# A recurrent decoder layer on one core: fifteen weight tiles split anew in every block instead of stored as parts, and neighbouring rows of w_in on a partition

## The chip, the core and the metric

The kernel runs on one core of one Trainium2 chip. The metric is the device time of one execution in microseconds (us). Five engines work side by side: PE (TensorE: matmuls, with its weight loads shown as PEld), DVE (VectorE), ACT (ScalarE), POOL (GpSimd) and SP (SyncE, which here only issues transfers); 16 DMA engines move the data. Each engine takes its instructions in the order of its own queue.

## The reference

One layer of a decoder on 2048 prompt tokens and 8 x 8 sample tokens. The input is normalised, one product with `w_in` (1024 x 8208) gives everything else, two branches (an RG-LRU with a causal convolution, and a gated delta rule) run over it, each is projected by its own matrix (`w_br_lru`, `w_br_gdn`), the two are weighed by sigmoid merge gates `m_lru`, `m_gdn` that are themselves 2 x 1024 columns of the input product, and `w_out` ends it.

```python
u = rms_norm(x, norm_pre)
z = jnp.einsum('btd,de->bte', u, w_in)
lru_x, lru_gate, gdn_qkv, gdn_gate, gdn_b, gdn_a, m_lru, m_gdn = jnp.split(z, offsets, axis=-1)
...
lru_out = h.astype(x.dtype) * jax.nn.silu(lru_gate)
...
p_lru = jnp.einsum('bte,ed->btd', lru_out, w_br_lru)
p_gdn = jnp.einsum('bte,ed->btd', gdn_out, w_br_gdn)
merged = jax.nn.sigmoid(m_lru) * p_lru + jax.nn.sigmoid(m_gdn) * p_gdn
y = jnp.einsum('btd,de->bte', merged, w_out)
x_new = x + rms_norm(y, norm_post)
```

All of it is float32. A float32 product is made of three products of a shorter format: each operand is split in a high part and the remainder, `hi` and `lo`, and `hi*hi + hi*lo + lo*hi` is summed (L545, L547, L549 in the kernel).

## The kernel before, in words

The 2048 prompt tokens go in four blocks of 512 (the loop `for blkno`); block 0 also takes the 64 sample tokens, so its moving operand has 576 columns and each weight tile is used in two halves of 256 and 320. In each block the same 88 weight tiles are used in the same order, `worder`. Places 0 to 15 alternate a K tile (one head's keys) and a merge-gate tile; 16 to 30 alternate the eight LRU input tiles and seven more merge-gate tiles; 31 to 34 are LRU gate tiles; 35 to 58 are q, v and gate tiles of the heads; 59 is the sixteenth merge-gate tile, 60 to 63 the other LRU gates, 64 to 79 the tiles of `w_br_gdn` and `w_br_lru`, 80 to 87 those of `w_out`.

A tile in its raw form is 1024 x 128 float32, 512 KB: 128 partitions of 8 rows each. Split, it is 1 MB. The matrices don't fit in the on-chip memory, so they pass through slots: three buffers `whl`, from block 1 on a fourth, `whx`, that takes every fourth tile (`wtile`).

- In block 0 `wload` fetches a raw tile (`raws`, or two neighbouring tiles as one `raw` of 1 MB), `split` (L203) writes `hi` by a Copy on ACT (its line in the profile is the helper's, L143) and `lo` by a subtraction on POOL (L205), and `wstore` (L275) writes the split tile, 1 MB, to a scratch tensor `dW` in DRAM: 88 stores. A tile's store is issued when the next tile is split (`wstore(1)`).
- In blocks 1 to 3 the slots are filled from `dW` (L300): 264 loads of 1 MB.

`proj` is one tile's work on PE: 8 steps of three matmuls. It takes a tile with `nextw`, calls `wfetch` for the tiles ahead, and hands the results to an evacuation on ACT or DVE. In block 0 that call also sets `A.after`: what ACT does next is ordered behind the split of the tile ahead ("weights first"). While the weights pass, PE is filled up with the products of the recurrent parts: `W.pump` doles out tasks by a cost table. What those tasks load and store through DRAM (`dk`, `dM`, `dD`, `dDT`, `er`, `dgc`) goes over SP's queue as well, in the order in which it was written, and so stands between the loads and stores of the weights.

The moving operand is the normalised input, transposed: `u_tile` (L348) turns token rows `ux` into channel rows by PE transposes (L196), eight groups `k` per block, scaled by `npre` as they leave PSUM. Group `k` holds channels `128k` to `128k+127`, as a raw tile holds rows `k*128+p` of `w_in` on partition `p`: the rearrangement in `wload` reads

```python
src[:, c:c + 128].rearrange("(k p) c -> p k c", p=128)
```

and `npre` is made of `norm_pre` by one more transpose at the start (`r0`).

## Time and profile before

| | us |
|---|---|
| three runs | 2682.43, 2687.51 (median), 2694.59 |
| the profiled execution | 2683.57 |
| its span | 2681.9 |
| PE busy (96 % of the span) | 2572.9 |
| DVE busy (56 %) | 1496.9 |
| ACT busy (33 %) | 885.3 |
| POOL busy (21 %) | 566.1 |
| stores `dW<-whl` | 88 of 1024 KB |
| loads `whl<-dW` and `whx<-dW` | 199 and 65 of 1024 KB |

How to read it: busy time is summed per engine, and an engine's idle time costs something only where it is on the path that sets the end. The chain that ended last runs over PE for 67 % of the span. Block 0 ends and block 1 begins at about 880 us; the four blocks are not alike, since only block 0 loads raw weights, splits and stores. The row of the granted TensorE clock over 40 slices reads 9 (90 % or more) nearly everywhere, and 8 in three slices between 134 and 335 us. The DMA row stands at 9 in several slices before 700 us.

### The profile page before, as it was taken

Reading aid. Unit: us, or ns where it says so; the run is one execution under the profiler, and the core shown is the slowest. Engines: PE = TensorE matmul, PEld = TensorE weight load, DVE = VectorE, ACT = ScalarE, POOL = GpSimd, SP = SyncE. Lnnn points to the kernel's source line nnn. Section 1 sums busy time; section 2 is a strip of 40 time slices with the busy share of each in tenths; the row PEclk is TensorE's granted clock in tenths of the full one; section 3 lists DMA queues with packets and bytes.
Section 4 is the critical chain, followed back from the end, with each engine's and each line's share of the span. In section 5 each row is a group of like instructions: output and inputs, shape, how many; then the busy total and the mean of one; then the engine's idle time right before and its main releaser. Section 6 shows DMA issues by size and latency. Waiting matters only on the chain.

```text
span 2681.9 us, 39949 instructions
## 1 busy us (share of the span) xinstructions
PE 2572.9 (96%) x15332; PEld 2238.6 (83%) x15332; DVE 1496.9 (56%) x3441; ACT 885.3 (33%) x1722; POOL 566.1 (21%) x444
## 2 busy tenths in 40 slices
PE   6888799999999999999999999999999999999999
PEld 5887798888999788888889788888889888888888
DVE  4567677787434557566523557566513458566512
ACT  5324543333324225323303235333303235333301
POOL 2443342232540211100110121100210211110200
PEclk9988899999999999999999999999999999999999
DMA  7987988789887887554466796544466886655465
GB/s 191 245 256 196 229 205 186 205 176 178 253 295 262 276 271 232 193 177 158 157 240 253 248 290 220 199 168 158 156 244 258 274 274 217 200 172 167 161 236 200
DMA packets 327897, 581.82 MB, mean 217 GB/s; under 512 B 70849, under 2 KB 236762, under 8 KB 282650
## 3 DMA queue, kind: packets, MB, share of 16 engines
q1 hardware_dynamic: 313882, 553.57, 67.0%
q10 hardware_dynamic: 13824, 25.70, 2.5%
q8 instruction: 121, 1.98, 0.3%
q14 instruction: 70, 0.57, 0.1%
HBM read 421.61 MB, written 157.59 MB: 216 GB/s over the span
## 4 chain that ended last, share of the span: by engine, by line
PE 67%; DMA 3%; issue 2%; DVE 1%; POOL 1%; ACT 1%; SPq 0%; ACTq 0%; POOLq 0%; DVEq 0%
PE mm L549 17%; PE mm L545 16%; PE mm L547 16%; PE g L192 5%; PE c L192 4%; PE mm L1284 2%; PE mm L1286 2%; PE mm L1288 2%; PE g L196 2%; DMA er<-dgc 1%; DMA dE<-er 1%; DMA dgc<-gr 0%; POOL er L746 0%; DVE cvy L576 0%; DMA ux<-in_x_prompt_dram 0%
## 5 line engine op out<-in xcount | busy, mean ns | idle before, releaser
L545 PE MATMUL mm<-a,whl 128*128 128x512 f32 (+2 forms) x2432 | 864.1, 355 | 25.5 <-ACT tmo L143 24.4
L549 PE MATMUL mm<-a,whl 128*128 128x512 f32 (+2 forms) x2432 | 868.7, 357 | 6.1 <-POOL whl L205 6.1
L547 PE MATMUL mm<-a,whl 128*128 128x512 f32 (+2 forms) x2432 | 862.8, 355 | 0.0
L545 PEld LDWEIGHTS mm<-a,whl 128*128 128x128 f32 x2432 | 465.5, 191 | 74.6 <-ACT tmo L143 26.1
L549 PEld LDWEIGHTS mm<-a,whl 128*128 128x128 f32 x2432 | 465.8, 192 | 59.3 <-POOL whl L205 6.7
L547 PEld LDWEIGHTS mm<-a,whl 128*128 128x128 f32 x2432 | 465.3, 191 | 45.8
L576 DVE SCALAR_TENSOR_TENSOR cvy<-cvr,cwg,cvy 128x512 f32<-128x512 f32 x288 | 220.0, 764 | 17.7 <-ACT cvy L143 12.4
L547 PE MATMUL mm<-a,whx 128*128 128x512 f32 x448 | 181.7, 406 | 0.0
L549 PE MATMUL mm<-a,whx 128*128 128x512 f32 x448 | 181.4, 405 | 0.0
L545 PE MATMUL mm<-a,whx 128*128 128x512 f32 x448 | 179.3, 400 | 0.0
L1222 DVE SCALAR_TENSOR_TENSOR pt<-tm,mm 128x512 f32<-128x512 f32 (+1 forms) x80 | 47.4, 592 | 189.6 <-PE mm L549 189.6
L1076 POOL TENSOR_TENSOR st<-st,mhalf 128x4 f32<-128x4 f32 x32 | 32.3, 1009 | 507.8 <-DVE st L1074 496.0
L143 ACT ACTIVATE cvr<-mm 128x512 f32<-128x512 f32 (+1 forms) x160 | 81.6, 510 | 172.3 <-PE mm L549 163.8
L205 POOL TENSOR_TENSOR whl<-raw,whl 128x1024 fp32r<-128x1024 f32 x44 | 108.5, 2467 | 121.4 <-ACT whl L143 107.0
L205 POOL TENSOR_TENSOR whl<-raws,whl 128x1024 fp32r<-128x1024 f32 x36 | 90.1, 2503 | 188.9 <-ACT whl L143 170.9
L1286 PE MATMUL mm<-whl,bt 128*128 128x256 f32 x448 | 126.4, 282 | 0.8 <-DVE whl L205 0.8
L1288 PE MATMUL mm<-whl,bt 128*128 128x256 f32 x448 | 126.3, 282 | 0.6 <-DVE yss L1262 0.6
L1284 PE MATMUL mm<-whl,bt 128*128 128x256 f32 x448 | 126.2, 282 | 0.0
L143 ACT ACTIVATE th<-cvy 128x512 f32<-128x512 f32 (+1 forms) x96 | 61.8, 644 | 188.3 <-DVE cvy L576 128.4
L143 ACT ACTIVATE yv<-c 128x128 f32<-128x128 f32 x128 | 35.5, 278 | 243.0 <-PE c L192 242.5
L549 PE MATMUL mm<-gp,whl 128*128 128x512 f32 (+2 forms) x296 | 104.2, 352 | 0.0
L545 PE MATMUL mm<-gp,whl 128*128 128x512 f32 (+2 forms) x296 | 104.1, 352 | 0.0
(331 smaller groups left out, 4645.9 us busy)
## 6 DMA issues: line engine op xcount, KB each, us to landing
whl<-dW SPq DMA_DIRECT2D x199, 1024.0 KB
dW<-whl SPq DMA_DIRECT2D x88, 1024.0 KB
whx<-dW SPq DMA_DIRECT2D x65, 1024.0 KB
raws<-in_w_in_dram SPq DMA_DIRECT2D x33, 512.0 KB
raw<-in_w_in_dram SPq DMA_DIRECT2D x15, 1024.0 KB
dtm<-tmo ACTq DMA_DIRECT2D x48, 256.0 KB
tm<-dtm SPq DMA_DIRECT2D x48, 256.0 KB
ux<-in_x_prompt_dram SPq DMA_DIRECT2D x16, 512.0 KB
```

The source lines that it names most:

```text
L143: r = f(*args, **kw)
L192: T.matmul(out, a, b, start=start, stop=stop)
L196: T.transpose(out, in_, idn)
L205: (eng or G).tensor_tensor(out=lo, in0=src, in1=hi.bitcast(F32), op=OP.subtract)
L545: T.matmul(ps[:, :n], wh, mh[:, c0:c0 + n], start=k == 0, stop=False)
L547: T.matmul(ps[:, :n], wh, ml[:, c0:c0 + n], start=False, stop=False)
L549: T.matmul(ps[:, :n], lo[:, k, :], mh[:, c0:c0 + n], start=False, stop=k == 7)
L576: V.scalar_tensor_tensor(out=y[:, :TB], in0=raw[:, i:i + TB], scalar=cw[:, i, ti:ti + 1], in1=y[:, :TB], op0=OP.mult, op1=OP.add)
L1222: proj(mov, lambda ps, c0, n: V.scalar_tensor_tensor(out=t_[:, c0:c0 + n], in0=x[:, c0:c0 + n], scalar=1.0, in1=ps[:, :n], op0=OP.add, op1 ...
L1284: T.matmul(ps[:, :256], mh[:, cs], wh[:, k % 4], start=k == 0, stop=False)
L1286: T.matmul(ps[:, :256], mh[:, cs], wl[:, k % 4], start=False, stop=False)
L1288: T.matmul(ps[:, :256], ml[:, cs], wh[:, k % 4], start=False, stop=k == 7)
```

## The change

Fifteen of the sixteen merge-gate tiles (`whole`: `mcol[:15]`, all but the one at place 59) are not stored in block 0. In blocks 1 to 3 they are loaded from `w_in` in raw form, two neighbouring tiles per transfer of 1 MB (the last alone, 512 KB: eight transfers per block), into the buffer `whx`, now called `wraw` there, and split into a `whl` slot again: an ACT Copy and a POOL subtraction per tile, 45 of each in all. `whx` serves no other tile at places up to 35 (`NP1`), and every fourth one behind; the split tiles at places up to 35 have the three `whl` buffers, and `proj` there asks for two tiles ahead and not three. The raw transfer of the next pair is issued by `wfetch` up to three tiles ahead.

Besides, rows of `w_in` are laid out the other way round (`krows`): partition `p` takes the eight neighbouring rows `8p` to `8p+7`, which in DRAM lie 32,832 bytes apart, where before it took rows `p`, `128+p`, and so on, 4,202,496 bytes apart. Each row piece is as long as before (512 bytes for a tile, 1 KB for a pair). So that the products stay the same, `u_tile` transposes every eighth channel of `ux` (a stride of 8 float32 along the row) and not 128 neighbouring ones, and `npre` is loaded directly in that layout; `r0`, its transpose and copy are gone. `w_br` and `w_out` tiles are laid out as before.

```diff
@@ -238,15 +238,20 @@
         wplace.setdefault(key(e), len(wplace))
     dW = [dram.tile([128, 2, 1024], F32, name=f"dW{i}") for i in range(len(wplace))]
     wstores, wraws = [], {}
+    NW, NP1 = len(wplace), paired[1]
+    whole = {key(e) for e in mcol[:8 + LM]}
+
+    def krows(a, by8):
+
+        return a.rearrange("(p k) c -> p k c", k=8) if by8 else a.rearrange("(k p) c -> p k c", p=128)
 
     wready = []
     wlast = [None]
     wnext, lnext = [0], [0]
-    ring, wx = [0], []
-
-    def wtile():
-        ring[0] += 1
-        if wx and ring[0] % 4 == 0:
+    wx = []
+
+    def wtile(n):
+        if wx and n % NW > NP1 and (n % NW - NP1) % 4 == 1:
             return wx[0].tile([128, 2, 1024], F32R, name="whx", tag="whx")
         return wp.tile([128, 2, 1024], F32R, name="whl", tag="whl", bufs=3)
 
@@ -260,15 +265,16 @@
             SP.dma_start(raw, src[c[1] * 512:(c[1] + 1) * 512, c[0] * 256:(c[0] + 1) * 256]
                          .rearrange("(k p) c -> p k c", p=128))
             wraws[key(e)] = raw
-        elif not (paired[0] <= n < paired[1] or paired[2] <= n < paired[3]):
+        elif not wx and not (paired[0] <= n < paired[1] or paired[2] <= n < paired[3]):
             raw = rw.tile([128, 8, 128], F32, name="raws", tag="raws")
-            SP.dma_start(raw, src[:, c:c + 128].rearrange("(k p) c -> p k c", p=128))
+            SP.dma_start(raw, krows(src[:, c:c + 128], src is win))
             wraws[key(e)] = raw
         else:
             two = [key(x) for x in worder[n:n + 7]].count((src.tensor.name, c + 128))
             w = 128 + 128 * two
-            raw = rp[0].tile([128, 8, w], F32, name="raw", tag="raw")
-            SP.dma_start(raw, src[:, c:c + w].rearrange("(k p) c -> p k c", p=128))
+            raw = (wx[0].tile([128, 8, w], F32, name="wraw", tag="whx") if wx else
+                   rp[0].tile([128, 8, w], F32, name="raw", tag="raw"))
+            SP.dma_start(raw, krows(src[:, c:c + w], src is win))
             for j in range(1 + two):
                 wraws[src.tensor.name, c + 128 * j] = raw[:, :, 128 * j:128 * j + 128]
 
@@ -279,13 +285,14 @@
             SP.dma_start(dW[i], hl.bitcast(F32))
 
     def wfetch(ahead):
+
 
         while wnext[0] < len(worder) and len(wready) < ahead:
             n = wnext[0]
             e = worder[n]
             place = wplace[key(e)]
             out = isinstance(e[1], tuple)
-            hl = wtile()
+            hl = wtile(n)
             hi, lo = (hl[:, j].rearrange("p (k c) -> p k c", c=256 if out else 128) for j in range(2))
             if n < len(wplace):
                 while lnext[0] < len(wplace) and lnext[0] <= n + (
@@ -294,10 +301,21 @@
                     lnext[0] += 1
                 wstore(1)
                 wlast[0] = split(hi, lo, wraws[key(e)], V if out else None)
-                wstores.append((place, hl))
+                if key(e) not in whole:
+                    wstores.append((place, hl))
+            elif key(e) in whole:
+                wstore()
+                wload(n)
+                split(hi, lo, wraws.pop(key(e)))
             else:
                 wstore()
                 SP.dma_start(hl.bitcast(F32), dW[place])
+            if wx:
+                for j in range(n + 1, min(n + 4, len(worder))):
+                    if key(worder[j]) in whole:
+                        if not any(x in wraws for x in whole):
+                            wload(j)
+                        break
             wready.append((hi, lo))
             wnext[0] += 1
 
@@ -351,7 +369,7 @@
             t = gtile()
             n = 0
             for xt, m in grp:
-                tr(t[:, n:n + m], xt[:m, k * 128:(k + 1) * 128], ident[:m, :m])
+                tr(t[:, n:n + m], xt[:m].rearrange("t (p k) -> t k p", k=8)[:, k], ident[:m, :m])
                 n += m
             cs = slice(gi * 512, gi * 512 + n)
             act(hi[:, cs], t[:, :n], AF.Copy, scale=npre[:, k:k + 1])
@@ -411,14 +429,10 @@
     with tc.tile_pool(name="init", bufs=2, side="right") as ip:
         rows = lambda a: a.rearrange("o (g p) -> (o g) p", p=128)
         with tc.tile_pool(name="u0", bufs=1) as up:
-            r0 = ip.tile([8, 128], F32, name="r0")
-            SP.dma_start(r0, rows(norm_pre))
+            SP.dma_start(npre, norm_pre.rearrange("o (p k) -> (o p) k", k=8))
             xh = u_load(0, up)
-            t = gtile()
-            tr(t[:, :8], r0, ident[:8, :8])
-            V.tensor_copy(npre, t[:, :8])
             wraw = ip.tile([128, 8, 16], F32, name="wraw", bufs=1)
-            SP.dma_start(wraw, win[:, C_B:C_B + 16].rearrange("(k p) c -> p k c", p=128))
+            SP.dma_start(wraw, krows(win[:, C_B:C_B + 16], True))
             u_norm(xh, up)
             zz = ip.tile([128, 96], F32, name="zz", bufs=1)
             V.memset(zz, 0.0)
@@ -526,7 +540,7 @@
         if blkno == 1:
             rw_cm.__exit__(None, None, None)
             wx.append(ctx.enter_context(tc.tile_pool(name="wx", bufs=1, side="right")))
-            ring[0] = 0
+            wraws.clear()
         sb = blkno == SB
         NB = TB + (NS if sb else 0)
         halves = [(0, 256), (256, 320)] if sb else [(0, 512)]
@@ -534,7 +548,7 @@
 
         def proj(mov, evac):
             w = nextw()
-            wfetch(3 if blkno else 1)
+            wfetch(1 if not blkno else 3 if wnext[0] % NW > NP1 else 2)
             A.after = wlast[0]
             hi, lo = w
             for c0, n in halves:
@@ -1262,7 +1276,7 @@
         V.memset(yss, 1.0)
         for q in range(4):
             ws = [nextw(), nextw()]
-            wfetch(2 if blkno else 1)
+            wfetch(2 if blkno and q < 3 else 1)
             order = [(i, k) for i in range(len(ntok)) for k in range(8)]
             if q == 0:
                 order = [(i, k) for i in (0, 1) for k in range(7)] + [(0, 7), (1, 7)] + order[16:]
```

The first place is SP's queue in block 0, from the store of the split K tile at place 8 (`dW_80` is place 0, so this is `dW_88`) to that of place 10; `dM`, `dk`, `dD`, `er` are transfers of the recurrent tasks. Before:

```order
L279 DMA dW_88<-whl 128x2048
L744 DMA er<-dgc 128x512
L498 DMA dD<-lru_877 128x4x128
L498 DMA dDT<-lru_877 128x4x128
L271 DMA raw<-in_w_in_dram 128x8x256
L770 DMA dM<-Mt 128x4x128
L279 DMA dW_89<-whl 128x2048
L797 DMA dk<-kT 128x576
L789 DMA dMs<-Ms 64x64
L498 DMA dD<-lru_877 128x4x128
L498 DMA dDT<-lru_877 128x4x128
L279 DMA dW_90<-whl 128x2048
```

Now:

```order
L285 DMA dW_88<-whl 128x2048
L512 DMA dDT<-lru_871 128x4x128
L784 DMA dM<-Mt 128x4x128
L758 DMA er<-dgc 128x512
L514 DMA dDs<-lru_871 64x8x64
L270 DMA raws<-in_w_in_dram 128x8x128
L811 DMA dk<-kT 128x576
L803 DMA dMs<-Ms 64x64
L270 DMA raws<-in_w_in_dram 128x8x128
L277 DMA raw<-in_w_in_dram 128x8x256
L285 DMA dW_90<-whl 128x2048
```

The store of the merge-gate tile at place 9 (`dW_89`) is gone, so that no store stands between the tiles 8 and 10, and other transfers of the tasks stand there.

The second place is POOL's queue at the start of block 1: `pt` and `yf` are the last of block 0, `er` the first of the recurrent tasks of block 1. Before:

```order
L1232 TENSOR_TENSOR pt_8353<-pt_8353,pt_8537 128x576
L341 TENSOR_TENSOR urr_8685<-uss_8684,mhalf_174 128x1 x2
L1301 TENSOR_TENSOR yf_9401<-yf_9401,mhalf_174 128x1 x5
L746 TENSOR_TENSOR er_9655<-er_9655,gcs_9446 128x512
L747 AFFINE_SELECT er_9655<-er_9655 128x512
L746 TENSOR_TENSOR er_9663<-er_9663,gcs_9446 128x512
L747 AFFINE_SELECT er_9663<-er_9663 128x512
```

Now:

```order
L1246 TENSOR_TENSOR pt_8334<-pt_8334,pt_8518 128x576
L359 TENSOR_TENSOR urr_8666<-uss_8665,mhalf_174 128x1 x2
L1315 TENSOR_TENSOR yf_9382<-yf_9382,mhalf_174 128x1 x5
L205 TENSOR_TENSOR whl_9466<-wraw_9467,whl_9466 128x1024
L205 TENSOR_TENSOR whl_9544<-wraw_9467,whl_9544 128x1024
L205 TENSOR_TENSOR whl_9629<-wraw_9547,whl_9629 128x1024
L760 TENSOR_TENSOR er_9641<-er_9641,gcs_9427 128x512
L761 AFFINE_SELECT er_9641<-er_9641 128x512
L760 TENSOR_TENSOR er_9649<-er_9649,gcs_9427 128x512
L761 AFFINE_SELECT er_9649<-er_9649 128x512
L775 TENSOR_TENSOR wk5_9434<-ssk_9714,phalf_176 128x4
L205 TENSOR_TENSOR whl_9764<-wraw_9547,whl_9764 128x1024
```

The subtractions of the merge-gate tiles at places 1, 3 and 5 stand ahead of the first `er`, that of place 7 behind two of them.

The third place is SP's queue at the same time, from the last output of block 0. `out_0` is the output, `dW0_80` to `dW4_84` the scratch tensors of places 0 to 4. Now:

```order
L1322 DMA out_0_dram<-y0_8689 128x512 x2
L1322 DMA out_0_dram<-y1_8690 128x512 x2
L277 DMA wraw_9467<-in_w_in_dram 128x8x256
L1322 DMA out_0_dram<-y2_8691 128x512 x2
L1322 DMA out_0_dram<-y3_8692 128x512 x2
L312 DMA whl_9471<-dW2_82 128x2048
L1322 DMA out_1_dram<-y4_8693 64x512 x2
L277 DMA wraw_9547<-in_w_in_dram 128x8x256
```

The first raw pair of block 1 takes the place that a load of `whx` from `dW` has before, behind the same four output transfers.

## Rows read from the trace of the kernel before

**Rows 1.** Windows, span: us, engines' busy us (instructions), granted clock, DMA share, GB/s

```profile
85.00:410.00 325.00, 271.91 (x1850) 263.68 (x1849) 210.76 (x532) 135.07 (x250) 128.22 (x83) 0.90 0.85 227
410.00:700.00 290.00, 273.35 (x2017) 243.42 (x2016) 219.78 (x527) 98.70 (x230) 82.42 (x47) 1.00 0.85 182
880.00:2682.00 1802.00, 1788.48 (x9694) 1500.40 (x9692) 953.54 (x2133) 548.31 (x1047) 261.86 (x246) 1.00 0.63 214
```

**Rows 2.** Waits of PE, 85 to 410: us in total, times, longest

```profile
PE mm L545 <- ACT tmo L143: 24.4, 8, 7.2
PE g L192 <- ACT lt L143: 8.6, 3, 5.8
PE mm L549 <- POOL whl L205: 6.1, 3, 5.3
PE g L192 <- ACT xh L143: 5.8, 1, 5.8
```

**Rows 3.** Waits of ACT, 85 to 410

```profile
ACT whl L143 <- DMA dW<-whl: 51.0, 10, 11.2
ACT er L143 <- POOL er L747: 38.5, 6, 12.5
...
ACT whl L143 <- DMA dDT<-lru: 10.1, 1, 10.1
```

**Rows 4.** Timeline of PE: start, duration, instruction, [idle before it, releaser]

```profile
98.68 0.63 PE L545 MATMUL mm<-a,whl 128*128 128x320 f32 x1 [7.19 <-ACT tmo L143]
```

**Rows 5.** Timeline of ACT at a split

```profile
207.29 1.06 ACT L143 ACTIVATE whl<-raw 128x1024 fp32r<-128x1024 f32 x1 [9.23 <-DMA dW<-whl]
```

**Rows 6.** Windows over four stretches at the lower clock; one, and their sum

```profile
93.40:103.60 10.20, 4.92 (x20) 4.92 (x21) 3.71 (x22) 4.20 (x8) 8.30 (x8) 0.50 0.87 291
...
sum 27.20, PE 20.01 PEld 20.02 DVE 17.93 ACT 8.78 POOL 15.64; mean PE 5.00 PEld 5.00 DVE 4.48 ACT 2.19 POOL 3.91
```

**Rows 7.** Windows of 20 us: w_in loads, w_br loads, scratch loads

```profile
620.00:640.00 20.00, 18.32 (x148) 17.08 (x146) 18.35 (x41) 7.44 (x16) 7.71 (x4) 1.00 1.03 153
720.00:740.00 20.00, 20.00 (x154) 20.00 (x153) 7.23 (x9) 4.88 (x5) 11.88 (x6) 1.00 1.00 351
1120.00:1140.00 20.00, 20.00 (x131) 16.70 (x130) 11.47 (x27) 5.34 (x12) 0.00 (x0) 1.00 0.42 134
```

**Rows 8.** Groups by line, ACT and POOL: count, busy, mean ns, idle before

```profile
L205 POOL TENSOR_TENSOR whl<-raw,whl 128x1024 fp32r<-128x1024 f32 x44 | 108.5, 2467 | 121.4 <-ACT whl L143 107.0 <-issue 9.8 <-DMA dgs<-gr 4.3
...
L143 ACT ACTIVATE whl<-raw 128x1024 fp32r<-128x1024 f32 x44 | 46.6, 1059 | 119.0 <-PE mm L549 48.0 <-DMA dW<-whl 46.4 <-DMA dDT<-lru 10.1
```

**Rows 9.** Waits of PE, 410 to 700

```profile
PE g L196 <- DVE cvy L591: 9.4, 7, 1.4
PE c L192 <- DVE S L1062: 6.8, 7, 1.3
```

**Rows 10.** Timeline of PE in block 0, first transposes

```profile
7.68 0.47 PE L196 MATMUL g<-ident,ux 128*128 128x128 f32 x1 [5.09 <-DVE ux L345]
```

**Rows 11.** Groups by form: PE's weight loads of the transposes

```profile
L196 PEld LDWEIGHTS g<-ident,ux 128*128 128x128 f32 x128 | 16.8, 158 | 16.8 <-ACT ux L143 7.5 <-DVE ux L345 5.2 <-DVE a L358 3.3
```

**Rows 12.** Groups by form: a strided copy on DVE

```profile
L816 DVE COPY invTT<-invT 128x1024 f32<-128x1024 f32 x4 | 4.4, 1110 | 0.1
```

**Rows 13.** Timeline of PE, transposes among w_out's products

```profile
1437.67 0.60 PE L196 MATMUL g<-ident,ux 128*128 128x128 f32 x4
1438.03 0.36 PE L1288 MATMUL mm<-whx,bt 128*128 128x256 f32 x1
```

**Rows 14.** Timeline of SP's DMA queue at the start of block 1

```profile
873.32 0.45 SPq L300 DMA_DIRECT2D whx<-dW  x1
```

**Rows 15.** Timeline of PE, first tile of block 1

```profile
881.60 0.39 PE L545 MATMUL mm<-a,whl 128*128 128x512 f32 x1
...
882.28 0.39 PE L545 MATMUL mm<-a,whl 128*128 128x512 f32 x1
```

**Rows 16.** Waits of POOL, block 1

```profile
POOL er L746 <- DMA er<-dgc: 53.8, 5, 30.2
```

## The prediction

> **What bounds the kernel now.** I read the profile page first: PE is busy 2572.9 of 2681.9 us, so the change can win only what PE idles, and what PE works at a lowered clock, unless it takes work off PE, which it hardly does. The windows by stage then say where that is. From 880 us on, blocks 1 to 3 leave 1802 - 1788.5 = 13.5 us of idle time in three blocks [rows 1]. Block 0 holds the rest: between 85 and 410 us, where K, LRU input and merge-gate tiles pass, PE idles 325 - 271.9 = 53 us, and the granted clock is 0.90 in the mean; from 410 to 700 it idles 16.7 us at a full clock.
>
> Third, what ends those waits. Of the 53 us, 24.4 + 8.6 + 6.1 + 5.8 = 44.9 end with ACT or with the subtraction of a split on POOL [rows 2]; DVE ends the other 8. ACT in turn waits, 61 us in eleven pieces, with the Copy of a split for a transfer out of the slot it is to write: 51 us of that for the store of the slot's earlier tile [rows 3]. One such place: the Copy at 207.29 takes 1.06 us and stood 9.23 us for a `dW<-whl` store [rows 5]. Because ACT is an in-order queue and its evacuations are ordered behind the split, PE then finds its PSUM buffers full: at 98.68 us it had stood 7.19 us for the evacuation `tmo` [rows 4]. So the chain in this stage is store, slot, split, evacuation, PE. The stores are late because the DMA engines are full: their share is 0.85 over the whole stage at 227 GB/s [rows 1].
>
> **The clock.** A mean of 0.90 over 325 us with a lower level of 0.50 means 325 x 0.10 / 0.50 = 65 us at the lower level (1.2 of 2.4 GHz). The stretch from 93.4 to 103.6 us, around the idle piece just named, is one of them [rows 6]. In the four stretches that I cut out PE is busy 20.0 of 27.2 us, 74 % [rows 6]; work done there would take half the time. So the lowered clock costs about 65 x 0.74 / 2 = 24 us. It falls around the gaps, and I take it to go in step with them.
>
> **The change, part by part.**
>
> *Fifteen stores less in block 0.* In 85 to 410 us the DMA engines are busy 0.85 x 325 = 276 us and move 227 x 325 = 73.8 MB [rows 1]. Some 13 of the 15 dropped stores lie in this stage, 13.6 MB; 60.2 MB are left. From the order of SP's queue: between the stores of K tiles 8 and 10 none is left, so about every second slot that a split writes had no store on it. That alone takes away half of the 44.9 us.
>
> *Neighbouring rows.* When the queue reads `w_in`, whose rows for a partition lie 4.2 MB apart, the engines are full (share 1.03) at 153 GB/s; reading `w_br` tiles with pieces of the same length but 4 KB apart they are full at 351; from scratch they give 134 at a share of 0.42, that is 319 at a full share [rows 7]. The first window also holds scratch traffic in short pieces, so not all of the factor is the distance. With rows 32,832 bytes apart I expect the upper kind of rate, 320 to 350: the 60.2 MB then keep the engines busy 172 to 188 us of the stage, not 276. The Trainium skill, "DMA: Bandwidth & Descriptors", section "Latency and other measured facts", gives a reason for this: it lists 207 GB/s at a pitch of 512 KiB between partitions, 164 at 2 MiB and 103 at 4 MiB. That is a pitch between partitions and not between the pieces of one, so it does not price this case; no run here shows it yet.
>
> With the engines a third less busy a remaining store lands sooner. I take it that half of the other half of the waits goes too: together three quarters of 44.9, **-34 us** of idle time (bounds -16 and -45). The clock follows in the proportion 34/53: **-15 us** (bounds -8 and -24). The 8 us that DVE ends stay.
>
> *410 to 700 us.* The engines are just as full there, but the 16.7 us of PE's idle time end with DVE (9.4 and 6.8 us in pieces of at most 1.4) [rows 9]. A faster transfer doesn't touch these: **0** (bound -16.7, if DVE itself ran late behind a load).
>
> *The start.* `r0` and its transpose go, but the first transposes of block 0 wait 5.09 us for DVE's normalised tokens [rows 10], which don't depend on it: **0**.
>
> *Transposes with a stride of 32 bytes.* 136 of them; 40 stand in block 0 at DVE's pace, 96 among the products of `w_out` in blocks 0 to 2. Four cost 0.36 us of PE's path [rows 13], the load of 128 columns 158 ns [rows 11]. No row shows a strided weight load. The nearest is a copy on DVE that writes with a stride of 128 bytes at 1110 ns per 1024 elements, one a cycle as if there were no stride [rows 12]. I take **0**, and as the bad end that a load takes as much again: 96 x 0.158 = +15 us.
>
> *Splits in blocks 1 to 3.* 45 times 1.06 us on ACT and 2.47 us on POOL [rows 8]. ACT and POOL are busy 548 and 262 of 1802 us there [rows 1]; 48 and 111 us more leave both with room. What counts is the slot. A tile's products take 8 x 0.68 = 5.5 us [rows 15]. With three `whl` buffers the slot for a merge-gate tile comes free two tiles, 11 us, before PE wants it; the split takes 3.5, so some 7 us are spare. The raw pair has the one buffer `wraw` and can start when both splits of the pair before are done, again some tiles ahead. Tightest is the first pair of block 1: its load takes the place of one that was issued at 873.32 [rows 14], and PE wants place 1 at 881.60 + 5.5 = 887.1 [rows 15]. A 1 MB pair takes 3.3 us at 320 GB/s, 6.9 at 153, the split 3.5: 880 to 884. If other loads share the engines it may be some us late, and PE then meets it once: **+3 us** (bounds -13.5, all idle time of the three blocks, which fewer loads could give, and +159, every split on the path). 22.5 MB fewer are moved; at a share of 0.63 nothing waits for them.
>
> **The sum.** -34 - 15 + 3 = -46. Against the profiled execution, 2683.57 us, that is **2638 us**. This execution lies 3.9 us below the median of the runs shown, 2687.51, so a median near 2640 would be no miss of the mechanism.
>
> **The rivals.**
>
> 1. *All of it goes.* No ACT or POOL wait is left in 85 to 410: -45 - 24 + 3 gives 2618, and 2612 if blocks 1 to 3 gain 3 rather than lose 3. For it: nearly each ACT wait in the stage ends with a transfer. Against: the recurrent tasks' own chain stays; ACT waits 38.5 us for POOL's `er` in the stage [rows 3]. Chance 0.12.
> 2. *The distance of the rows does not matter*, and only the dropped stores count. Half of the waits lose their store, but part of that is taken by the next thing in line, the raw pair that is as slow as before: -16 idle, -8 clock, +3 gives 2662. For it: the slow window [rows 7] is also full of short task transfers. Chance 0.13.
> 3. *Strided weight loads cost as much again*, +15: 2653. The Trainium skill, "SBUF — State Buffer", section "Door 1: The DMA port swizzle", speaks against the change here: it says that on-chip lines are 16 bytes and each access that crosses to a new line pays, so that float32 strides beyond four elements are not free, and these are eight. By that rule the sum would be 2653; by the DVE row it is 2638, and no row shows such a load on PE. Chance 0.10.
> 4. *Slower: the subtraction stands on the path in blocks 1 to 3.* POOL takes things in order, and in block 1 it waits 53.8 us for `er` transfers, once 30.2 us [rows 16]; in the new order the subtraction of place 7 stands behind two `er`. If every merge-gate tile met that, 45 x 2.47 = 111 us: 2638 - 3 + 111 = 2746. The break-even is 49/45 = 1.1 us exposed per tile. Against it: three subtractions stand ahead of the first `er`, and 7 us are spare per tile. Chance 0.07.
> 5. *No effect.* The tasks' `er` chain keeps ACT as late as the stores did, and PE's gaps change their releaser, not their length: 2675 to 2686. Chance 0.06.
>
> **How the numbers follow.** The forecast has 0.52. The range 2612 to 2670 leaves out the slower case, most of no effect and a little at the ends; its upper end is rival 2 with half of the strided cost. A measurement here can tell a change from none at about 0.5 %, 13.4 us, so faster means below 2674: the forecast and rivals 1 to 3, 0.87, less 0.03 for sums of their bad ends, 0.84. Same is rival 5 and those 0.03: 0.09. Slower is rival 4: 0.07.
>
> **What the changed profile would show.** If right: PE's idle time in 85 to 410 us falls from 53 to about 19, with the granted clock near 0.96; ACT's wait for `dW<-whl` falls to a quarter; a stretch like 620 to 640, engines full, moves well over 153 GB/s; the transposes' loads stay near 158 ns; blocks 1 to 3 idle some 17 us, with at most one wait of a few us on a split of `wraw`. Wrong: an unchanged GB/s at a full share (rival 2), transposes' loads near 300 ns (rival 3), PE waits `<- POOL whl` spread over blocks 1 to 3 (rival 4), PE waits in 85 to 410 that now follow `er` or DVE (rival 5).

## The result, and the profile after

The change made the kernel slower: 2771.43 us (median of four runs, 2768.86 to 2776.32) against 2685.11 before (also the median of four, the three runs shown above among them), a ratio of 1.0324, 95 % interval 1.0308 to 1.034. The forecast was 2638, the range 2612 to 2670.

The blocks can be timed by the sixteen products with `wst` at the head of each. In these rows of the changed kernel (durations in ns, then the first and the last start in us) a block's time runs from one first start to the next:

```profile
L192 PE MATMUL mm<-a,wst x16: 389/393/404, 838.7 to 842.2; 128*128 128x512 f32 x16
...
L192 PE MATMUL mm<-a,wst x16: 387/396/404, 1483.4 to 1486.9; 128*128 128x512 f32 x16
...
L192 PE MATMUL mm<-a,wst x16: 387/396/404, 2125.6 to 2129.1; 128*128 128x512 f32 x16
```

| stage | before | after | difference |
|---|---|---|---|
| block 0 (up to those products) | 877.9 | 838.7 | -39.2 |
| block 1 | 602.0 | 644.7 | +42.7 |
| block 2 | 601.0 | 642.2 | +41.2 |
| block 3, to the end | 601.0 | 642.3 | +41.3 |
| span | 2681.9 | 2767.9 | +86.0 |

So block 0 gained most of what was forecast (-49), and blocks 1 to 3, forecast at +3, lost 125 us, evenly. The windows of the changed kernel, as in [rows 1]:

```profile
85.00:410.00 325.00, 289.97 (x2099) 280.21 (x2098) 241.73 (x606) 147.86 (x281) 140.08 (x89) 0.95 0.80 198
410.00:700.00 290.00, 275.44 (x2040) 249.81 (x2040) 203.93 (x471) 99.77 (x220) 100.51 (x56) 1.00 0.82 202
838.70:2767.90 1929.20, 1821.66 (x9704) 1519.75 (x9702) 1025.44 (x2138) 590.65 (x1094) 369.95 (x291) 0.97 0.60 189
```

PE's idle time in 85 to 410 us is down from 53 to 35 us at a clock of 0.95. In blocks 1 to 3 it is up from 13.5 to 107.5 us, and the granted clock, 1.00 before, is 0.97. Taken over the same products in both kernels (877.9 to 2681.9 us before), 94 of the 125 us are more idle time of PE, and 31 are more busy time for as many matmuls, at the lower clock. PE's waits there, by releaser (us in total, times, longest):

```profile
PE mm L559 <- DMA whl<-dW: 57.4, 16, 8.4
PE mm L559 <- ACT er L143: 20.2, 2, 10.7
PE g L196 <- DVE rr L526: 11.8, 1, 11.8
```

None of the larger ones ends with a split. PE waits for split tiles that come late from scratch, and for recurrent tasks (`er`, `rr`). Here is one such place: SP's queue, then PE, then the load in the chain of work that ended last (start, duration):

```profile
919.62 0.60 SPq L277 DMA_DIRECT2D wraw<-in_w_in_dram  x1
922.35 0.33 SPq L811 DMA_DIRECT2D dk<-kT  x1
922.77 2.18 SPq L312 DMA_DIRECT2D whl<-dW  x1
```

```profile
938.51 0.77 PE L559 MATMUL mm<-a,whl 128*128 128x512 f32 x1 [6.89 <-DMA whl<-dW]
```

```profile
922.77 15.60 DMA whl<-dW
```

A raw pair is issued at 919.62, the load of a split tile behind it at 922.77; that load lands 15.6 us later, and PE has stood 6.89 us for it. By the packet records the pair's own pieces fill 921.0 to 934.3 us.

In block 0 the waits of ACT for a `dW` store, 51 us in [rows 3], are gone entirely. Still PE idles 35 us, and these are PE's and ACT's largest waits in 85 to 410 us:

```profile
PE mm L559 <- ACT tmo L143: 11.5, 2, 11.1
PE g L192 <- ACT xh L143: 9.4, 2, 4.9
PE mm L559 <- ACT cvy L143: 5.0, 2, 4.4
```

```profile
ACT er L143 <- POOL er L761: 38.4, 6, 11.8
ACT xh L143 <- DVE cvy L596: 21.6, 5, 7.7
...
ACT th L143 <- DVE cvy L596: 15.8, 5, 4.7
```

ACT stands for POOL's `er` as long as before (38.4 us for 38.5 in [rows 3]) and for DVE's convolutions (`cvy`) twice as long, 37.4 us in these two rows. Before, the two were

```profile
ACT th L143 <- DVE cvy L582: 10.4, 3, 4.0
...
ACT xh L143 <- DVE cvy L582: 7.7, 3, 4.8
```

### The profile page after: what moved, and what is told of

The parts are those of the page before. It is cut to its first block, busy times and chain, and to the rows that moved or that the text cites. A ratio compares the mean times of both kernels' runs of the same rounds, so it can differ in the third digit from the quotient of the medians.

```text
span 2767.9 us, 39973 instructions
## 1 busy us (share of the span) xinstructions
PE 2588.7 (94%) x15331; PEld 2243.7 (81%) x15331; DVE 1566.8 (57%) x3440; ACT 926.8 (33%) x1767; POOL 674.4 (24%) x489
## 4 chain that ended last, share of the span: by engine, by line
PE 58%; DVE 5%; DMA 5%; issue 3%; POOL 2%; SPq 2%; ACT 1%; ACTq 0%; POOLq 0%; DVEq 0%
PE mm L563 14%; PE mm L559 14%; PE mm L561 14%; PE g L192 4%; PE c L192 4%; DMA whl<-dW 3%; PE mm L1298 2%; PE mm L1300 2%; PE mm L1302 2%; PE g L196 2%; DVE invT L827 1%; DVE invt L825 1%; SPq L840 1%; DVE cvy L590 1%; POOL whl L205 1%
## 5 line engine op out<-in xcount | busy, mean ns | idle before, releaser
L559 PE MATMUL mm<-a,whl 128*128 128x512 f32 (+2 forms) x2640 | 954.0, 361 | 95.4 <-DMA whl<-dW 57.4
L563 PE MATMUL mm<-a,whl 128*128 128x512 f32 (+2 forms) x2640 | 955.3, 362 | 0.0
L561 PE MATMUL mm<-a,whl 128*128 128x512 f32 (+2 forms) x2640 | 950.7, 360 | 0.0
L559 PEld LDWEIGHTS mm<-a,whl 128*128 128x128 f32 x2640 | 507.6, 192 | 160.5 <-issue 56.8
L563 PEld LDWEIGHTS mm<-a,whl 128*128 128x128 f32 x2640 | 507.2, 192 | 63.1 <-issue 5.1
L561 PEld LDWEIGHTS mm<-a,whl 128*128 128x128 f32 x2640 | 507.6, 192 | 55.6
L590 DVE SCALAR_TENSOR_TENSOR cvy<-cvr,cwg,cvy 128x512 f32<-128x512 f32 x288 | 241.9, 840 | 18.6 <-ACT cvy L143 13.1
L205 POOL TENSOR_TENSOR whl<-wraw,whl 128x1024 fp32r<-128x1024 f32 x45 | 112.1, 2490 | 200.8 <-ACT whl L143 175.6
L563 PE MATMUL mm<-gp,whl 128*128 128x512 f32 (+2 forms) x296 | 104.2, 352 | 0.0
L559 PE MATMUL mm<-gp,whl 128*128 128x512 f32 (+2 forms) x296 | 104.1, 352 | 0.0
L561 PE MATMUL mm<-gp,whl 128*128 128x512 f32 (+2 forms) x296 | 104.0, 351 | 0.0
L561 PE MATMUL mm<-a,whx 128*128 128x512 f32 x240 | 98.9, 412 | 0.0
```

The source lines that it names most:

```text
L205: (eng or G).tensor_tensor(out=lo, in0=src, in1=hi.bitcast(F32), op=OP.subtract)
L559: T.matmul(ps[:, :n], wh, mh[:, c0:c0 + n], start=k == 0, stop=False)
L561: T.matmul(ps[:, :n], wh, ml[:, c0:c0 + n], start=False, stop=False)
L563: T.matmul(ps[:, :n], lo[:, k, :], mh[:, c0:c0 + n], start=False, stop=k == 7)
L590: V.scalar_tensor_tensor(out=y[:, :TB], in0=raw[:, i:i + TB], scalar=cw[:, i, ti:ti + 1], in1=y[:, :TB], op0=OP.mult, op1=OP.add)
```

## The experiments

Seventeen kernels were run, each beside the kernel before on the same chip. The two last columns are the times of block 0 and of blocks 1 to 3 together in one profiled execution, by the `wst` products as above; they can differ from the medians by a few us. In four of the kernels (one raw load per block, with three slots and with four, and the aligned source, with three and with four) the merge gates get wrong weights: these only show where time goes.

| run | median us | ratio to before, interval | block 0 | blocks 1-3 |
|---|---|---|---|---|
| before | 2685.1 | | 877.9 | 1804.0 |
| the change | 2771.4 | 1.0324 (1.0308 to 1.0340) | 838.7 | 1929.2 |
| row layout alone | 2668.4 | 0.9949 (0.9934 to 0.9964) | 860.4 | 1802.9 |
| whole tiles alone | 2798.8 | 1.0437 (1.0419 to 1.0455) | 844.6 | 1956.8 |
| slots alone | 2679.5 | 0.9991 (0.9982 to 1.0000) | 861.6 | 1814.6 |
| one raw load per block | 2688.1 | 1.0024 (1.0013 to 1.0035) | 837.1 | 1846.5 |
| two raw buffers | 2757.8 | 1.0285 (1.0269 to 1.0300) | 836.3 | 1918.1 |
| repacked | 2736.1 | 1.0203 (1.0188 to 1.0218) | 872.8 | 1862.6 |
| repacked, two buffers | 2737.2 | 1.0211 (1.0194 to 1.0228) | 870.6 | 1861.5 |
| raw on ACT's queue | 2733.7 | 1.0198 (1.0179 to 1.0218) | 839.2 | 1892.0 |
| splits unread | 2766.0 | 1.0320 (1.0305 to 1.0335) | 858.4 | 1905.5 |
| aligned source | 2703.6 | 1.0087 (1.0070 to 1.0103) | 838.8 | 1863.2 |
| repacked late, two buffers | 2729.9 | 1.0183 (1.0168 to 1.0198) | 862.9 | 1861.1 |
| raw loads unread | 2702.1 | 1.0066 (1.0040 to 1.0092) | 861.9 | 1837.3 |
| four slots | 2747.0 | 1.0244 (1.0228 to 1.0259) | 839.7 | 1907.9 |
| four slots, one raw load | 2650.8 | 0.9885 (0.9868 to 0.9901) | 838.6 | 1809.4 |
| four slots, ACT's queue | 2765.0 | 1.0301 (1.0278 to 1.0324) | 846.0 | 1917.8 |
| four slots, aligned source | 2675.0 | 0.9970 (0.9958 to 0.9983) | 838.9 | 1837.0 |
| four slots, raw form stored | 2673.8 | 0.9964 (0.9952 to 0.9976) | 859.0 | 1815.0 |

### The parts of the change

**The row layout alone**, made from the kernel before:

```diff
-            SP.dma_start(raw, src[:, c:c + w].rearrange("(k p) c -> p k c", p=128))
+            SP.dma_start(raw, krows(src[:, c:c + w], src is win))
...
-                tr(t[:, n:n + m], xt[:m, k * 128:(k + 1) * 128], ident[:m, :m])
+                tr(t[:, n:n + m], xt[:m].rearrange("t (p k) -> t k p", k=8)[:, k], ident[:m, :m])
...
```

> The kernel before with the new row layout alone (w_in rows 8p to 8p+7 on a partition, strided transposes, npre loaded directly); all 88 tiles stored and loaded as before. Stages by the start of the blocks: before, block 0 takes 878 us and blocks 1 to 3 together 1804; the change 839 and 1929. Theory A (raw transfers of w_in in blocks 1 to 3 hold up what is issued behind them): blocks 1 to 3 stay at 1804 within 10 us; block 0 keeps only the gain at the start, some 10 us; total about 2675. Theory D (the layout is what costs, by the strided transposes or the reads): blocks 1 to 3 lose part of the 125 us, total above 2720.

It takes 2668.4 us and is faster than the kernel before by 0.5 %: blocks 1 to 3 are unchanged and block 0 is shorter by 17.5 us. The strided transposes are not what costs. These are the window of the stage 85 to 410 us and ACT's wait for stores in it:

```profile
85.00:410.00 325.00, 282.12 (x1957) 272.03 (x1957) 224.13 (x562) 140.00 (x263) 131.56 (x85) 0.93 0.86 234
```

```profile
ACT whl L143 <- DMA dW<-whl: 52.3, 12, 10.2
```

The engines move 234 GB/s at a share of 0.86, 272 for a full share, where before it was 267: neighbouring rows read no faster to speak of, and the store waits are as long as before (52.3 us for 51.0). PE idles 43 us all the same, not 53. Why, these runs do not show.

**The whole tiles alone**, the change without the layout:

```diff
-            SP.dma_start(raw, krows(src[:, c:c + w], src is win))
+            SP.dma_start(raw, krows(src[:, c:c + w], False))
...
```

> The change without the new row layout: the fifteen tiles unstored and split in every block, rows of w_in and transposes as before. Theory A: blocks 1 to 3 lose as much as in the change, 1900 to 1960 us, since the packets of w_in tiles were as slow in block 0 in either layout; total 2750 to 2790. Theory D: blocks 1 to 3 come back to about 1810, total near 2650.

It takes 2798.8 us, so the loss belongs to the whole tiles. In the change, with the layout added, blocks 1 to 3 are 28 us shorter than here.

**The slots alone** (nothing whole, row layout, slots and look-ahead of the change):

```diff
-    whole = {key(e) for e in mcol[:8 + LM]}
+    whole = set()
...
```

> The change with nothing kept whole: all tiles stored and loaded as before, but with its slots (no fourth buffer at places up to 35) and its look-ahead of two tiles there. Theory C (the loss is the lost buffer and shorter look-ahead): blocks 1 to 3 take over 1880 us. Theory A: 1800 to 1825 us. Block 0 goes back to about 870, since the stores are there again.

Blocks 1 to 3 take 1814.6 us against the layout's 1802.9: the lost buffer and the shorter look-ahead cost 12 us by themselves.

### Splits or loads

**One raw load per block:**

```diff
-                wload(n)
-                split(hi, lo, wraws.pop(key(e)))
+                if n % NW == 1:
+                    wload(n)
+                    reuse[0] = wraws.pop(key(e))
+                split(hi, lo, reuse[0])
...
-                        if not any(x in wraws for x in whole):
-                            wload(j)
```

> The change, but in blocks 1 to 3 only the first of the eight raw transfers of a block is made, and all fifteen splits of the block read that pair (so fourteen merge-gate tiles have the wrong columns); the splits on ACT and POOL, the slots and the look-ahead stay. Theory A: blocks 1 to 3 take 1805 to 1840 us (one late pair per block), total 2650 to 2680. Theory B (the splits themselves stand on the path): still over 1900, total over 2740.

It takes 2688.1 us, and blocks 1 to 3 1846.5: 83 of the 125 us go with seven of eight raw transfers, while all 45 splits stay. Six waits make up PE's larger ones in the three blocks:

```profile
PE mm L560 <- DMA whl<-dW: 17.2, 3, 6.6
PE g L192 <- ACT xh L143: 16.4, 3, 5.5
```

**Two raw buffers:**

```diff
-wx[0].tile([128, 8, w], F32, name="wraw", tag="whx")
+wx[0].tile([128, 8, w], F32, name="wraw", tag="whx", bufs=2)
```

> The change with a second buffer for the raw pairs, so that the transfer of the next pair needn't wait on SP's queue for the split of the pair before; which transfers are made, and from where, stays. With the change, blocks 1 to 3 take 1929 us, and SP stands 52 us in block 1 for POOL's split. Theory A1 (it is SP's wait for the single buffer, with all that stands behind it): blocks 1 to 3 fall to 1850 or less, total under 2700. Theory A2 (it is the transfer itself, slow pieces of w_in that fill the DMA engines and hold up what is issued behind): 1890 to 1930, total 2735 to 2775.

Blocks 1 to 3 take only 11 us less. But this does not show that SP's wait is harmless: each raw transfer came to stand a pair further ahead, and SP still stood for POOL's splits at the start of block 1, 40.5 us where it was 52.1 in the change:

```profile
SPq L277 <- POOL whl L205: 40.5, 6, 15.6
```

**The raw transfers on ACT's queue**, with two buffers:

```diff
-            SP.dma_start(raw, krows(src[:, c:c + w], src is win))
+            (A if wx else SP).dma_start(raw, krows(src[:, c:c + w], src is win))
```

> Two raw buffers, and the raw transfers of blocks 1 to 3 issued from ACT's queue, not SP's: the slow pieces of w_in then stand in another queue than the loads of split tiles and the transfers of the tasks. If what hurts is that transfers behind a raw pair in the same queue land after it, blocks 1 to 3 fall to 1850 or less, total under 2700. If it is the DMA engines' time that the slow pieces take, whatever the queue, no more than 20 us under the run with two buffers on SP's queue.

Blocks 1 to 3 take 1892.0 us, 26 less than with two buffers on SP's queue, so between the two expectations. Here the queue that issues the transfers is a part of the loss, not the whole.

**Splits that nobody reads**, added to the slots run, with one raw load per block:

```diff
...
+                hx = wx[0].tile([128, 2, 1024], F32R, name="whd", tag="whd")
+                split(*(hx[:, j].rearrange("p (k c) -> p k c", c=128) for j in range(2)), reuse[0])
```

> The slots run (all tiles stored and loaded, the slots, look-ahead and row layout of the change) with the 45 splits of blocks 1 to 3 added, written to a buffer that nobody reads, and one raw transfer per block for them; PE waits for none of it. The slots run took 1815 us for blocks 1 to 3, the run with one raw load per block, whose splits PE does need, 1846. Theory O (the 48 us of ACT and 111 us of POOL disturb the recurrent tasks' own use of these in-order queues): 1835 to 1855. Theory B (PE waits for the split itself): 1815 to 1825. Total 2680 to 2720.

It takes 2766.0 us, and blocks 1 to 3 91 us more than in the slots run; that is more than the splits that PE does need cost anywhere. The run has a fault of its own: its one spare buffer makes each Copy wait for the subtraction before, and ACT's queue with it, 22.5 us in 862 to 1100 us:

```profile
ACT whd L143 <- POOL whd L205: 22.5, 11, 2.6
```

Whether this wait is what costs the 91 us was not tried. The run says nothing of the change's splits, which have no such buffer; a later run with four slots bears on those.

### What is slow in the raw loads

**Repacked:** the merge-gate columns are copied once to a scratch where each partition's part is contiguous.

```diff
+            if 64 <= n < NW and (n - 64) % 3 == 0:
+                i = (n - 64) // 3
+                c0 = pairs[i][0][1]
+                SP.dma_start(dR[i], krows(win[:, c0:c0 + 128 * len(pairs[i])], True))
...
-            SP.dma_start(raw, krows(src[:, c:c + w], src is win))
+            SP.dma_start(raw, dR[[p[0][1] for p in pairs].index(c)] if wx else krows(src[:, c:c + w], src is win))
```

> The change with the raw columns of the merge-gate tiles copied once, in eight transfers from DRAM to DRAM late in block 0 (places 64 to 85), to a scratch where a partition's part is contiguous; blocks 1 to 3 load their raw pairs from there. Bytes, splits, slots and SP's waits stay. Theory A2: blocks 1 to 3 fall from 1929 to 1820 to 1860 us, block 0 grows from 839 by 0 to 15; total 2665 to 2710. Theory A1: 1900 or more, total above 2735.

Blocks 1 to 3 fall by 67 us to 1862.6, close to what the theory of slow pieces had. Block 0 loses 34 us, more than expected. The copies did not stay late (first and last start in the row, 117.7 and 329.4 us):

```profile
L303 SPq DMA_DIRECT2D dR<-in_w_in_dram x8: 528/1037/2417, 117.7 to 329.4; - x8
```

**Repacked, with two buffers** (both edits):

> Both: the repacked scratch and two raw buffers. Theory A2: as with the scratch alone, less at most 15 us. Theory A1: as with two buffers alone. If each holds a part, the parts add up to nearly the whole loss: blocks 1 to 3 at 1810 to 1830, total 2650 to 2680.

Blocks 1 to 3 take 1861.5 us: the second buffer adds nothing here.

**Repacked late, with two buffers**, the copies ordered behind the splits of places 64 to 85 on ACT's queue:

```diff
-                SP.dma_start(dR[i], krows(win[:, c0:c0 + 128 * len(pairs[i])], True))
+                A.after = wlast[0]
+                A.dma_start(dR[i], krows(win[:, c0:c0 + 128 * len(pairs[i])], True))
```

> The repacked scratch with two raw buffers, with the eight copies ordered behind the splits of places 64 to 85 on ACT's queue: in the repacked runs the scheduler had put them between 118 and 329 us, where block 0 lost 32 us. Block 0 back to 840 to 855, blocks 1 to 3 at 1860 as before: total 2705 to 2720, still slower than the kernel before by about 1 %.

It takes 2729.9 us, above the expected range; the copies now start between 653 and 820 us, and block 0 still pays 24 us against the change.

**An aligned source:** the same number of 1 KB pieces, from a matrix whose rows lie 4096 bytes apart (so the merge gates get other weights).

```diff
-            SP.dma_start(raw, krows(src[:, c:c + w], src is win))
+            SP.dma_start(raw, krows(w_br_gdn[0][:, c // 128 % 6 * 128:c // 128 % 6 * 128 + w] if wx else src[:, c:c + w], src is win))
```

> The change, but in blocks 1 to 3 the raw pairs are read from the w_br_gdn matrix, whose rows lie 4096 bytes apart, in pieces of the same 1 KB (the merge gates get wrong weights). With w_in blocks 1 to 3 take 1929 us, with a contiguous copy 1863. If it is w_in's layout in DRAM (rows of 32,832 bytes) that makes the pieces slow, blocks 1 to 3 take 1850 to 1880, total 2690 to 2715. If it is the small piece or the number of pieces, 1910 to 1930, total 2755 to 2775.

Blocks 1 to 3 take 1863.2 us, the same as from the contiguous copy. In the 18.8 us from the issue of the raw pair at 919.6 us the change's window reads

```profile
919.60:938.40 18.80, 12.02 (x58) 9.75 (x56) 7.70 (x20) 3.36 (x5) 1.01 (x1) 0.89 0.92 176
```

and in the same stretch of the aligned run, from its issue at 912.6 us,

```profile
912.60:931.40 18.80, 18.80 (x92) 15.63 (x92) 9.92 (x23) 5.63 (x9) 7.15 (x6) 1.00 0.81 278
```

The DMA engines move 176 GB/s at a share of 0.92 in the change, and 278 at 0.81 here. By the packet records of the traces, a 1 KB piece takes 120 ns in the mean between 900 and 1100 us with `w_in` and 56 with the aligned source, at a median of 46 in both: some pieces are slow, not all. PE's waits of the aligned run in blocks 1 to 3, against 57.4, 20.2 and 11.8 us in the change:

```profile
PE mm L559 <- DMA whl<-dW: 17.4, 7, 5.4
...
PE mm L559 <- ACT er L143: 6.1, 2, 3.9
PE g L196 <- DVE rr L526: 5.4, 1, 5.4
```

**Raw loads that nobody reads**, added to the row layout alone, on SP's queue at the places of the change's raw loads, each behind the load of a split tile (45 MB of loads from scratch that the change leaves out stay in):

```diff
+                if wx and n % NW in (0, 3, 7, 11, 15, 19, 23, 27):
...
+                    hx = wx[0].tile([128, 8, w], F32, name="whd", tag="whd")
+                    late.dma_start(hx, krows(win[:, c0:c0 + w], True))
```

> The run with the row layout alone (all tiles stored and loaded, four slots, look-ahead of three; 2668 us, blocks 1 to 3 in 1803), with the eight raw transfers from w_in per block added at their places in SP's queue, into a spare buffer that nobody reads; no split, no wait on a split. Theory L (the slow transfers themselves make the loads of split tiles behind them land late): blocks 1 to 3 take 1840 to 1890, with PE's waits ending at loads of whl from the scratch; total 2705 to 2755. Theory R (PE loses because the raw data of its own split are late, and SP stands for the splits): 1800 to 1820, total 2665 to 2685.

Blocks 1 to 3 take 1837.3 us, 34 over the layout alone and just under the range; and PE's wait is not where it was expected:

```profile
PE g L192 <- DVE kT L598: 21.4, 10, 5.1
```

`kT` is a task's tile, written by DVE. No wait of PE ends at a load of `whl`: with four slots none comes too late. So the slow transfers cost in two places: split tiles that come late, and tasks that do.

### Cover

**Four slots:** a fourth buffer for split tiles beside the raw one, and three tiles of look-ahead.

```diff
+        if wx and n % NW <= NP1 and n % 4 == 3:
+            return wx[0].tile([128, 2, 1024], F32R, name="why", tag="why")
...
-            wfetch(1 if not blkno else 3 if wnext[0] % NW > NP1 else 2)
+            wfetch(3 if blkno else 1)
```

> The change with its cover given back: a fourth slot for split tiles at places up to 35 beside the raw buffer, and a look-ahead of three tiles there. The raw loads, splits and SP's waits stay. Theory K (the thin cover lets late loads of split tiles reach PE): blocks 1 to 3 fall from 1929 to 1860 to 1890 us, PE's waits for whl from the scratch from 57 to under 20, total 2700 to 2730. Theory W (SP stands for the splits of the pair before, whatever the slots): still 1910 or more, total over 2750.

Blocks 1 to 3 take 1907.9 us, far from the 1860 to 1890 of thin cover and next to the other theory's 1910. PE's waits for `whl` are gone (57.4 to 2.3 us), and most of the time went to the tasks instead:

```profile
PE g L192 <- DVE kT L607: 56.3, 10, 8.3
PE g L196 <- DVE rr L528: 6.7, 1, 6.7
...
PE mm L561 <- DMA whl<-dW: 2.3, 2, 1.2
```

One of them, on DVE and on PE:

```profile
895.03 0.29 DVE L528 COPY rr<-g 128x128 f32<-128x128 f32 x1 [10.17 <-DMA out_dram<-rr]
```

```profile
895.37 0.42 PE L196 MATMUL g<-ident,shg 128*64 128x128 f32 x1 [6.73 <-DVE rr L528]
```

DVE stood 10.17 us for a store of `rr` to land, and PE 6.73 us for DVE behind it. More cover moves the wait; the late transfers remain.

**Four slots, one raw load per block** (both edits, so again fourteen tiles with wrong columns):

> The same with one raw load per block, as in the earlier run of that kind (1846 us for blocks 1 to 3 with three slots; merge gates get wrong weights). Theory K: 1810 to 1830, total 2645 to 2670, which would leave 10 to 25 us to the splits themselves. If the splits on ACT and POOL cost by themselves, it stays near 1846.

It takes 2650.8 us, and blocks 1 to 3 1809.4, 6.5 over the layout alone, with all 45 splits read by PE. Its largest waits in the three blocks:

```profile
PE g L192 <- ACT xh L143: 5.4, 6, 1.6
PE g L196 <- ACT zr L143: 1.4, 1, 1.4
```

So with four slots the splits cost little where no slow transfer is near. The 6.5 us are a balance, since 45 loads of 1 MB from scratch are gone; PE idles 11.8 us in these blocks of the layout run, and fewer loads can't give back more idle time than that. An estimate from the two: the splits cost at most some 18 us.

**Four slots, the raw loads on ACT's queue:**

> As the first of these, with the raw loads issued from ACT's queue. If both parts hold: blocks 1 to 3 at 1835 to 1870, total 2675 to 2710, so at best near the kernel before; if ACT's in-order queue loses what SP's gains, no faster than the first.

It takes 2765.0 us, and blocks 1 to 3 take 10 more than with the raw loads on SP's queue: the 26 us that ACT's queue gained with three slots and two raw buffers are not there with four slots.

**Four slots, aligned source:**

> The four-slot version with the raw pairs of blocks 1 to 3 read from w_br_gdn (rows of 4096 bytes, pieces of the same 1 KB; merge gates get wrong weights). With w_in blocks 1 to 3 take 1908 us, without seven of the eight loads 1809. If the slowness of w_in's pieces is nearly all of it: 1810 to 1835, total 2650 to 2680. If any megabyte in SP's queue delays the tasks' transfers as much: 1870 or more, total over 2710.

It takes 2675.0 us, and blocks 1 to 3 1837.0, a little over the range; PE's wait for `kT` falls from 56.3 to 16.7 us:

```profile
PE g L192 <- DVE kT L607: 16.7, 6, 4.2
```

**Four slots, the raw form stored once** in block 0, 512 KB a tile and not 1 MB, and loaded back from that contiguous scratch:

```diff
-                    wstores.append((place, hl))
+                    wstores.append((dW[place], hl.bitcast(F32)))
+                else:
+                    i, j = rplace[key(e)]
+                    wstores.append((dR[i][:, j].rearrange("p (k c) -> p k c", c=128), wraws[key(e)]))
...
```

> The four-slot version with each merge-gate tile's raw form stored once in block 0 (512 KB, not 1 MB), and the raw pairs of blocks 1 to 3 loaded from that contiguous scratch. Block 0 between the change's 839 and the 860 of the row layout with all stores: 845 to 855. Blocks 1 to 3 as with the aligned source, 1810 to 1835. Total 2655 to 2690: it beats the kernel before if the contiguous loads cost under 30 us, and the row layout alone (2668) only at the lower end.

It takes 2673.8 us. Blocks 1 to 3 take 1815.0, with this left of the `kT` wait:

```profile
PE g L192 <- DVE kT L620: 5.8, 6, 1.6
```

Block 0 takes 859.0, though, as long as with all stores at full size (860.4). This version beats the kernel before by 0.4 %, and is no better than the row layout alone, the fastest of the versions that leave nothing out.

## Why the prediction was wrong

**The step that failed** is "Splits in blocks 1 to 3", the +3, and in it the sentence that 22.5 MB fewer are moved and nothing waits for them. It counted bytes and the slot of the merge-gate tile itself, and took the time of a raw pair (3.3 to 6.9 us) as the pair's own affair. By the packet records the four pairs between 900 and 1100 us took 7.2 to 13.3 us each. And the step should have asked what stands behind a slow transfer in SP's queue, as the part on block 0 did. The term measured +126 against the row layout alone. The four-slot runs split it in steps:

- from 1802.9 to 1809.4 with all splits and one raw load (+7);
- to 1837.0 with all eight loads a block, in fast pieces (+28);
- to 1907.9 with the pieces of `w_in` (+71);
- to 1929.2 with three slots and the shorter look-ahead (+21).

From a contiguous scratch the +28 is +6 (1815.0). The loss is the transfers, by their slow pieces above all.

What is open: the same slow loads cost 34 us unread and 99 us (1907.9 less 1809.4) when splits depend on them. One candidate is SP, which issues nothing while it waits for the splits of the pair before. By itself it is not this: SP stands as long with the raw form stored as with the pieces of `w_in`, both with four slots, and the first has blocks of 1815.0 us. The second row is that of the raw form stored:

```profile
SPq L279 <- POOL why L205: 82.9, 18, 9.8
```

```profile
SPq L284 <- POOL why L205: 92.2, 19, 8.9
```

What the unread loads lack besides is a split that stands in ACT's and POOL's queues between the tasks' own work. The four-slot run shows one such place, its longest wait for `kT`, and the chain that leads up to it:

```profile
2212.25 1.01 PE L192 MATMUL g<-kT 128*128 128x128 f32 x3 [8.32 <-DVE kT L607]
```

```profile
2185.27 15.80 DMA er<-dgc
...
2202.23 2.38 POOL whl L205
2204.61 0.60 POOL er L763
...
2205.23 0.64 ACT er L143
```

A transfer of a task, issued 4.4 us behind a raw pair (2180.87), lands after 15.8 us. POOL then makes the subtraction of a split between two steps of `er`, and ACT's evacuations, DVE's `kT` and PE come behind it. How much of the 99 us arises this way no run tells.

**The splits themselves** went as argued where no slow transfer is near. The subtraction took 2.49 us (2.47 in [rows 8]), and with four slots and one raw load the blocks are 7 us over the layout. The slower rival, subtractions behind `er`, had a chance of 0.07 and the right sign; its cause is wrong in the main. No larger wait of PE ends with POOL in the change, and the subtraction on the path just shown adds 2.4 us to a delay that a transfer made.

```profile
L205 POOL TENSOR_TENSOR whl<-wraw,whl 128x1024 fp32r<-128x1024 f32 x45 | 112.1, 2490 | 200.8 <-ACT whl L143 175.6 <-DMA gwr<-in_lru_wa_dram 21.0 <-DMA out_dram<-y 4.3
```

**Neighbouring rows** were forecast at 320 to 350 GB/s; the layout run shows 272 for a full share, 267 before. So rival 2's premise, that the distance of the rows does not matter, held in this stage; in blocks 1 to 3, with the raw loads, the layout was worth 28 us (1956.8 to 1929.2). The slow window of [rows 7] was a sign about `w_in` itself, not about the distance of the rows on one partition: with the aligned source pieces of the same size are fast. The Trainium skill's figures for pitches between partitions ("DMA: Bandwidth & Descriptors", "Latency and other measured facts") start at 512 KiB; the pitch between partitions went from 32,832 to 262,656 bytes here and the rate hardly changed, so no run tests them.

**Block 0** gained 39.2 where 49 was forecast: 17.5 by the layout, 21.7 more by the stores. The clock's term came out: for as many matmuls, PE's busy time in block 0 fell by 15.3 us, where -15 was forecast. The idle term did not: forecast -34, measured -24 over block 0 (95.6 to 71.7 us of idle time), of it 18 in the stage from 85 to 410 us (53 to 35). The store waits went to zero, not to a quarter, and still PE gained only half. (Of the eleven pieces of ACT's wait that the prediction counted, one of 10.1 us in [rows 3] ends with a transfer of a task, `dDT`, and not with one out of the slot.) What is left follows the tasks' own chain (`er`, convolutions), as in rival 5; this is read from the waits, and no run tried it.

**The transposes:** the strided weight load takes 198 ns where it took 158 [rows 11]:

```profile
L196 PEld LDWEIGHTS g<-ident,ux 128*128 128x128 f32 x128 | 18.4, 198 | 16.2 <-DVE uss L358 7.9 <-ACT ux L143 7.0 <-DVE a L376 0.5
```

The Trainium skill, "SBUF — State Buffer", section "Door 1: The DMA port swizzle", was right that such a stride is not free, where the DVE row had suggested it. At 96 x 0.04 = 4 us it does not matter here, and the blocks of the layout run show none of it.

## What to carry to other kernels

Fewer bytes are no gain where the new transfer is slower per byte and others stand behind it on the same queue: price a transfer by how long those behind it are held up, and name them. Before a tile is fetched again from a source matrix in every pass, look at what that matrix reads at a full DMA share; here a contiguous copy brought 1908 us to 1815, but storing that copy cost block 0 19 us of the 22 that dropping the stores had gained. And give back the cover (slots, look-ahead) that a new buffer displaces, or the change is judged with a second one mixed in.

## What the runs showed of the hardware that was not expected

Pieces of 1 KB read from a matrix with rows of 32,832 bytes kept the DMA engines busy for more than twice as long as the same pieces from rows of 4096 bytes (120 ns against 56 in the mean, 900 to 1100 us). The order of the rows over the partitions changed little: in 85 to 410 us the mean was 114 ns before and 101 with neighbouring rows, in 900 to 1100 us 129 in the whole tiles alone and 120 in the change. Whether it is the alignment of the pieces or where the rows lie in memory was not tried. A float32 weight load with a stride of 32 bytes took 25 % longer than a contiguous one (198 ns against 158).
